# Attention times values in plain float32, two heads on the two column halves of TensorE

## The chip, the cores and the metric

The kernel runs on one core of a Trainium2 chip. A core has a matrix engine (TensorE, PE in the profile; its weight loads are PEld), three engines for elementwise work (VectorE or DVE, ScalarE or ACT, GpSimd or POOL), and SyncE (SP), which issues most of the DMA transfers. Each engine works through its own queue in order and waits on semaphores for the others. The metric is the device time of one execution in microseconds (us).

## The reference

One step of a streaming encoder layer. A prompt of 2048 frames and a sample of 8 x 16 frames, both 1024 wide, are normalised and projected by one input matrix; three groups of heads of width 64 read the result, and one output matrix merges them:

- A: 6 heads; a frame sees its own chunk of 64 frames and the 8 chunks before, with a learned bias by distance.
- B: 6 query heads on 2 key/value heads; own chunk and 2 chunks before, a linear distance bias, and a learned sink per head.
- M: 4 heads of cross-attention into 256 memory tokens.

```python
def _attn_core(q, k, v, bias, valid, sink):
    s = jnp.einsum('...qhgd,...khd->...hgqk', q, k).astype(jnp.float32) * SCALE
    ...
        p = jax.nn.softmax(s, axis=-1)
    ...
    return jnp.einsum('...hgqk,...khd->...qhgd', p.astype(v.dtype), v)


def _merge(x, oa, ga, ob, gb, om, gm, w_out, g_post):
    o = jnp.concatenate([oa * jax.nn.silu(ga), ob * jax.nn.silu(gb), om * jax.nn.silu(gm)], axis=-1) @ w_out
    return x + _rmsnorm(o, g_post)
```

All data are float32. The change is about the second einsum, p times v, for the prompt.

## The kernel before, in words

**Groups and steps.** The prompt is cut into 4 groups of 512 frames; group 0 also carries the 128 sample rows. In each group the kernel projects with the input matrix (`project_T`, line 191, gives 128 columns of q, k or a gate for all frames, transposed; `project_N`, line 202, gives rows of v, and the output projection), attends, and projects out. The order within a group is written out by hand in `ORDERS` (line 42): `V` projects values, `Pa`/`Pb` project q, k and gate of a pair of heads, `Aa`/`Ab`/`M` attend, `X` loads a pair's context, `L` loads and scales the next group's rows, `Q` projects the next group's M queries, `F` finishes the rows of the group before. A tile framework then schedules every engine's queue from this order with a simulated timeline, so later work can fill in where earlier work is not ready. The last part of a group is mostly attention, and the output projection follows it.

**Precision by splitting.** Most products run in the format that the code calls `F32R`. For them the code splits an operand into a high part (a copy to F32R) and a low part (the difference), and adds up products: three passes for a projection (high x high, high x low, low x high). Input weights are split by `load_w`: a DMA into `wraw`, a copy on ScalarE (line 139), a subtraction on VectorE or GpSimd (line 140), into one of three `whl` buffers.

**Attention of a pair of heads.** Two heads h = 0, 1 share a 128-partition tile, 64 rows each. For A the 512 queries are taken in two sub-steps of 2 x 128 (`for i0 in (0, 2)`); for B and M all 512 at once.
- Scores (line 241) go to PSUM, one tile `s` at a time. VectorE adds the bias and takes the minimum (lines 727, 798; 643 for M), ScalarE takes the exponential (729, 800, 648), VectorE scales by the reciprocal (732, 809, 653). The weights stand in `sb` tiles, of which there are five buffers.
- `transposed_p` turns up to four 128 x 128 blocks of one head on TensorE (line 247) into a PSUM tile `pt` (three buffers). Then `split`: ScalarE copies the high part (208), VectorE subtracts for the low part (209), both into one of three `pslot`s.
- Values are stored per head as 128 columns: high part and low part of 64 columns each, arranged so that head 0 has its high part in columns 0 to 63 and head 1 in columns 64 to 127. `attend` (line 260) multiplies the 128-column value block once with the high and once with the low weights, all into one PSUM tile `o`: two matmuls for each head and value block, of 256 columns (a block that two query tiles see) or 128 columns (one query tile).
- The two column halves of the result have to be added: `merge` copies one half to `sums` on ScalarE (267) and adds the other on VectorE (268), per head. `gate` multiplies `sums` with the SiLU gate on GpSimd (631) into `mo`.

**Output.** `split_mixed` (890 on VectorE, 891 on GpSimd) splits `mo` into `mixhl`, and `project_out` multiplies. The last group has its own code (lines 914 to 959) that begins the output projection before the last pair is done; it splits four output weight tiles ahead, two of them into spare room, two into `whl` buffers.

**One shared region.** `sh` (10496 columns) holds, at different times and overlapping, keys, four value slots, the three `pslot`s, the memory split `memhl` and `mixhl`. Context keys and values of A go to DRAM (`kctx_d`, `vctx_d`) and come back one group later by GpSimd's DMA queue (lines 840, 841).

**The sample rows** (`sample_attn`) already use plain float32: line 358 multiplies with 32-column stationary blocks, one for each of four sequences b, each into its own 32 partitions of the PSUM tile, and line 392 does the same for the values, for every block t of 128 cached frames. Line 385 transposes.

Of the kernel before, what the change touches and what calls it, by code (L numbers as in the profile page):

```python
# [9 lines left out]
F32 = mybir.dt.float32  # L10
# [39 lines left out]
def encoder_step(ctx, tc, x_p, x_s, xT0, xT, mem, memT, wt, wm, g_pre, g_mem, g_post, rel_rev, sink,  # L50
# [10 lines left out]
    sbp = ctx.enter_context(tc.tile_pool(name="sbp", bufs=5))  # L61
    cp_ = ctx.enter_context(tc.tile_pool(name="cp", bufs=1))
# [10 lines left out]
    sh = cst.tile([128, 10496], F32R, name="sh")  # L73
# [10 lines left out]
    def region(off, *dims):  # L84
        n = int(np.prod(dims))
        ap = sh[:, off:off + n]
        names = "abcde"[:len(dims)]
        if len(dims) > 1:
            pat = " ".join(names)
            ap = ap.rearrange(f"p ({pat}) -> p {pat}", **dict(zip(names[1:], dims[1:])))  # L90
        return ap


    keys = region(0, 2, 1664)
    kslot = [keys[:, :, 128 + 512 * i:640 + 512 * i] for i in range(3)]
    pslot = [region(7424 + 1024 * i, 2, 512) for i in range(3)]
    mixhl = region(0, 5, 2, KB, 128)
    memhl = region(0, 2, KB, 256)
    mixlast = xn[:, :8192].rearrange("p (i a k r) -> p i a k r", i=4, a=2, k=KB)
    turn = {"p": 0, "s": 0, "q": 0, "g": 0, "d": 0, "u": 0, "m": 0}  # L100

    def vregion(slot):
        return sh[:, 3328 + 1024 * slot:4352 + 1024 * slot].rearrange("p (a b) -> p a b", b=256)
# [17 lines left out]
    mV = cst.tile([128, 2, 2, 256], F32R, name="mV")  # L121
# [6 lines left out]
    vctx_d = [drp.tile([128, 4, 256], F32, name=f"vctx{i}") for i in range(6)]  # L128
# [55 lines left out]
    def project_T(w, src, c0, n, ps=None):  # L184

        if ps is None:
            ps = p_mm.tile([128, 512], F32, tag="mm", name="psT")
        i = 0
        for k in range(KB):
            for a, b in ((0, 0), (0, 1), (1, 0)):  # L190
                pe.matmul(ps[:, :n], w[:, a, k * 128:(k + 1) * 128], src[:, b, k, c0:c0 + n],  # L191
                          start=(i == 0), stop=(i == 23))
                i += 1
        return ps
# [48 lines left out]
    def transposed_p(blocks):  # L243
# [5 lines left out]
        dst = pslot[1 + turn["p"] % 2 if turn["m"] else turn["p"] % 3]  # L249
        turn["p"] += 1  # L250
        split(dst[:, 0, :n], dst[:, 1, :n], pt[:, :n])
        return dst

    def attend(o, items, first):

        n = 2 * len(items)
        i = 0
        for v, pt, c, w, oc in items:
            for part in range(2):
                pe.matmul(o[:, oc:oc + w], v, pt[:, part, c:c + w], start=(first and i == 0), stop=(i == n - 1),  # L260
                          skip_group_check=True)
                i += 1

    def merge(o, h, col, dst, n):

        m, x = slice(64 * h, 64 * h + 64), slice(64 - 64 * h, 128 - 64 * h)
        act.activation(dst[m, :n], o[x, col:col + n], AF.Copy)
        dve.tensor_tensor(dst[m, :n], o[m, col:col + n], dst[m, :n], ALU.add)  # L268
# [12 lines left out]
    def memory_rows(cols):  # L281

        for k in range(KB):
            act.activation(memhl[:, 0, k], cols[k], AF.Copy, scale=gmem[:, k:k + 1])
            dve.scalar_tensor_tensor(memhl[:, 1, k], cols[k], gmem[:, k:k + 1], memhl[:, 0, k].bitcast(F32),
                                     ALU.mult, ALU.subtract)
# [15 lines left out]
    def memory_keys(st):  # L302
# [11 lines left out]
        for i in range(2):  # L314
            ps = project_N(ws, lambda a, k: memhl[:, a, k, i * 128:(i + 1) * 128])
            split_v([mV[:, 0], mV[:, 1]], i, ps, st[:, i:i + 1])
# [175 lines left out]
    def project_out(ws, c, i, gpost, st):  # L492

        ps = project_N(ws, lambda a, k: mixhl[:, i, a, k])
# [22 lines left out]
    def xg(g):  # L517
        return xnT[min(g, 1)]
# [60 lines left out]
    mst = memory_rows(mT)  # L579
    qg.append((*block_q(0, 7, w7[0]), block_g(0, 7, w7[1])))  # L580
    memory_keys(mst)
# [5 lines left out]
    for g in range(NG):  # L587
# [14 lines left out]
        def block_v(slots, half):  # L602
            ws = [weights("v", half, r) for r in range(2)]
            for i in range(5 if g == 0 else 4):
                ps = project_N(ws, lambda a, k: xg(g)[:, a, k, i * 128:(i + 1) * 128])
# [9 lines left out]
                split_v(slots, i, ps, rs_rows[:, i:i + 1] if g == 0 else None)  # L615
# [12 lines left out]
        def gate(f, col, n, sums, G, g=g):  # L628

            dst = mom[:, f - 6, col // 128:(col + n) // 128] if f > 5 and g else mo[:, col // 128:(col + n) // 128, f]  # L630
            pool.tensor_tensor(dst, sums[:, :n].rearrange("p (a b) -> p a b", b=128),  # L631
                               G[:, col:col + n].rearrange("p (a b) -> p a b", b=128), ALU.mult)


        def attn_m(g, pr, q, Q, G):
            f = 6 + pr
            sums = cp_.tile([128, 512], F32, tag="sums", name="sums")
            for h in range(2):
# [5 lines left out]
                sbs = []  # L644
                for i2 in range(2):
# [8 lines left out]
                    sbs.append(sb)  # L654
                o = p_o.tile([128, 512], F32, tag="o", name="om")
                for i2 in range(2):
                    pt = transposed_p([sbs[i2][:, i * 256 + j * 128:i * 256 + (j + 1) * 128]
                                       for j in range(2) for i in range(2)])
# [428 lines left out]
```

## Time and profile before

| | |
|---|---|
| median of 3 runs | 1199.81 us (1195.86 to 1201.51) |
| the profiled execution, own time | 1199.29 us |
| its span | 1197.5 us |
| TensorE matmuls, busy | 1137.5 us, 95% |
| VectorE, busy | 840.0 us, 70% |
| ScalarE, busy | 689.5 us, 58% |
| GpSimd, busy | 362.2 us, 30% |

How to read it. A row of a group of instructions gives line, engine, operation, the tile written and the tiles read, the shapes, the count, then busy us and mean ns of one, then the idle time of the engine just before them and what ended it. Busy time by stage gives, for a stretch of the span, each engine's busy us and number of instructions, then TensorE's granted clock, the DMA share and GB/s. The chain of waits goes back from the last instruction to whatever released each step; its shares say which work set the end. In the timeline a row gives start, length, engine, line and count; matmuls overlap, so their pace is the distance of starts.

### The profile page before, as it was taken

How to read it: one execution, taken by the hardware profiler on the slowest of the kernel's cores; microseconds unless marked ns; L12 is line 12 of the kernel's file. 1: busy time of each engine (PE TensorE's matmuls, PEld its weight loads, DVE VectorE, ACT ScalarE, POOL GpSimd, SP SyncE). 2: the span in 40 equal slices, each digit the busy share in tenths (PEclk: the TensorE clock that was granted, in tenths of full speed). 3: DMA queues.
4: the chain of work that ended last, by engine and by line, in shares of the span. 5: the costliest groups of instructions: out<-in, count | busy, mean ns of one | idle time of the engine just before them, and what ended most of it. 6: DMA issues, size and time to landing. Idle time of an engine off the chain costs nothing.

```text
span 1197.5 us, 20992 instructions
## 1 busy us (share of the span) xinstructions
PE 1137.5 (95%) x7794; PEld 1024.5 (86%) x7794; DVE 840.0 (70%) x1911; ACT 689.5 (58%) x1609; POOL 362.2 (30%) x286
## 2 busy tenths in 40 slices
PE   7899999999989999999999999999988998999897
PEld 6789898897679988898888988898778987988797
DVE  7648666777784457779997336679997336679965
ACT  6546565655544565558664455557765444667652
POOL 5411210211261552122433552122333450221441
PEclk9899999999889999999999999999999998999999
DMA  7673552624621593333311493333321471432213
GB/s 264 211 226 130 172 181 57 232 83 151 240 71 53 176 341 119 110 111 112 126 58 36 133 360 115 111 114 123 115 63 36 129 285 54 126 97 89 90 54 106
DMA packets 62239, 163.43 MB, mean 136 GB/s; under 512 B 8109, under 2 KB 19379, under 8 KB 62137
## 3 DMA queue, kind: packets, MB, share of 16 engines
q1 hardware_dynamic: 58392, 152.66, 38.4%
q0 software_dynamic: 3744, 9.44, 2.7%
q8 instruction: 61, 1.00, 0.3%
q14 instruction: 42, 0.34, 0.1%
HBM read 140.95 MB, written 23.48 MB: 137 GB/s over the span
## 4 chain that ended last, share of the span: by engine, by line
PE 74%; DVE 16%; ACT 3%; issue 3%; DMA 2%; POOL 1%; SPq 0%; DVEq 0%; POOLq 0%; ACTq 0%
PE psT L191 33%; PE psN L202 23%; PE pt L247 5%; PE oa L260 4%; PE sa L241 3%; DVE sh L209 3%; DVE whl L140 1%; DVE sba L727 1%; PE om L260 1%; DVE sbb L798 1%; DVE sbb L809 1%; PE ss L358 1%; PE so L392 1%; PE ob L260 1%; PE sm L241 1%
## 5 line engine op out<-in xcount | busy, mean ns | idle before, releaser
L191 PE MATMUL psT<-xn,whl 128*128 128x512 f32 (+2 forms) x2400 | 531.8, 370 | 11.3 <-ACT whl L139 6.8
L191 PEld LDWEIGHTS psT<-xn,whl 128*128 128x128 f32 x2400 | 410.1, 192 | 73.9 <-ACT whl L139 7.1
L140 POOL TENSOR_TENSOR whl<-wraw,whl 128x1024 fp32r<-128x1024 f32 x64 | 155.7, 2433 | 357.5 <-ACT whl L139 303.7
L202 PE MATMUL psN<-whl,sh 128*128 128x256 f32 x1296 | 162.2, 283 | 1.5 <-POOL sh L891 1.3
L202 PEld LDWEIGHTS psN<-whl,sh 128*128 128x128 f32 x1296 | 156.4, 189 | 3.7 <-POOL sh L891 1.5
L139 ACT ACTIVATE whl<-wraw 128x1024 fp32r<-128x1024 f32 (+1 forms) x132 | 138.2, 1047 | 33.8 <-PE psN L202 13.7
L202 PE MATMUL psN<-whl,xn 128*128 128x256 f32 x1080 | 143.0, 283 | 3.1 <-ACT stgN L618 1.1
L202 PEld LDWEIGHTS psN<-whl,xn 128*128 128x128 f32 x1080 | 133.4, 189 | 7.2 <-issue 1.6
L209 DVE TENSOR_TENSOR sh<-pt,sh 128x512 fp32r<-128x512 f32 (+2 forms) x206 | 123.7, 625 | 21.5 <-ACT sh L208 20.5
L208 ACT ACTIVATE sh<-pt 128x512 fp32r<-128x512 f32 (+2 forms) x206 | 104.4, 547 | 41.0 <-PE pt L247 34.0
L729 ACT ACTIVATE sba<-sba,sta 128x640 f32<-128x640 f32 (+4 forms) x96 | 73.1, 761 | 65.8 <-DVE sta L727 64.0
L140 DVE TENSOR_TENSOR whl<-wraw,whl 128x1024 fp32r<-128x1024 f32 (+1 forms) x68 | 98.9, 1455 | 15.8 <-ACT whl L139 15.4
L631 POOL TENSOR_TENSOR mo<-sums,gr 128x256 f32<-128x256 f32 (+1 forms) x44 | 45.0, 1022 | 186.3 <-DVE sums L268 169.0
L727 DVE CUSTOM_DVE_ANT_0 sba<-sa,nbA 128x640 f32<-128x640 f32 (+4 forms) x96 | 70.6, 735 | 33.2 <-PE sa L241 32.4
L260 PE MATMUL oa<-sh 128*128 128x256 f32 (+1 forms) x504 | 82.0, 285 | 10.9 <-DVE sh L209 7.7
L260 PEld LDWEIGHTS oa<-sh 128*128 128x128 f32 x504 | 71.5, 192 | 17.0 <-DVE sh L209 9.6
L497 DVE TENSOR_TENSOR mo<-psN,gpost 128x256 f32<-128x256 f32 x52 | 22.1, 424 | 73.8 <-ACT junk L496 73.7
L247 PE MATMUL pt<-ident,sba 128*128 128x128 f32 x420 | 67.5, 281 | 3.4 <-DVE sba L732 3.2
L800 ACT ACTIVATE sbb<-sbb,stb 128x256 f32<-128x256 f32 (+1 forms) x96 | 47.3, 493 | 27.7 <-DVE stb L798 27.5
L732 DVE TENSOR_SCALAR sba<-sba,sta 128x640 f32<-128x640 f32 (+4 forms) x96 | 59.9, 624 | 2.6
L496 ACT ACTIVATE junk<-psN 128x256 bf16<-128x256 f32 x52 | 20.0, 384 | 62.3 <-PE psN L202 62.2
L247 PEld LDWEIGHTS pt<-ident,sba 128*128 128x128 f32 x420 | 49.6, 143 | 7.1 <-DVE sba L732 4.2
(282 smaller groups left out, 1643.9 us busy)
## 6 DMA issues: line engine op xcount, KB each, us to landing
wraw<-in_wt SPq DMA_DIRECT2D x128, 512.0 KB, 3.6
xr<-in_x_p SPq DMA_DIRECT2D x16, 512.0 KB, 5.8
nbA<-skew_d SPq DMA_DIRECT2D x24, 320.0 KB, 3.2
vta<-in_cva SPq DMA_DIRECT2D x12, 512.0 KB, 4.5
xt<-in_x_p SPq DMA_DIRECT2D x12, 512.0 KB, 5.0
out_y_p<-mo SPq DMA_DIRECT2D x12, 512.0 KB, 4.7
vctx<-sh SPq DMA_DIRECT2D x9, 512.0 KB, 5.4
kctx<-sh SPq DMA_DIRECT2D x9, 512.0 KB, 4.1
```

The source lines that it names most:

```text
L139: act.activation(hl[:, 0, m], raw[:, m], AF.Copy)
L140: eng.tensor_tensor(hl[:, 1, m], raw[:, m], hl[:, 0, m].bitcast(F32), ALU.subtract)
L191: pe.matmul(ps[:, :n], w[:, a, k * 128:(k + 1) * 128], src[:, b, k, c0:c0 + n], start=(i == 0), stop=(i == 23))
L202: pe.matmul(ps[:, :256], stat(a, k), w[:, b, (k % 4) * 256:(k % 4 + 1) * 256], start=(k == ks[0] and i == 0), stop=(k == ks[-1] and i == 2))
L208: act.activation(hi, src, AF.Copy)
L209: eng.tensor_tensor(lo, src, hi.bitcast(F32), ALU.subtract)
L241: pe.matmul(out[:, c:c + n], q[:, part, qc:qc + 128], kt[:, h, kc:kc + n], start=part == h, stop=part != h)
L247: pe.transpose(pt[:, i * 128:(i + 1) * 128], b, ident)
L260: pe.matmul(o[:, oc:oc + w], v, pt[:, part, c:c + w], start=(first and i == 0), stop=(i == n - 1), skip_group_check=True)
L727: dve.tensor_tensor_reduce(sb[:, :nk], s[:, c0:c0 + nk], nb[h][:, 640 - nk:], 1.0, 3.0e38, ALU.add, ALU.min, st[:, e:e + 1])
L729: act.activation(sb[:, :nk], sb[:, :nk], AF.Exp, bias=st[:, e:e + 1], scale=-1.0, accum_out=st[:, 2 + e:3 + e])
L732: dve.tensor_scalar(sb[:, :nk], sb[:, :nk], st[:, 4 + e:5 + e], 0.5, ALU.mult, ALU.mult)
```

## The change

The products of weights and values for the prompt take plain float32 operands. Nothing is split there: `transposed_p` only copies, `keep_v` stores the values once. The two heads' products go to the two column halves: head h uses the 64 value columns of its own as stationary block and writes partitions 64h to 64h + 63 of `o`. So the result needs no `merge`, and `gate` multiplies straight from PSUM, on VectorE. Blocks of both heads now share a transposed tile, all transposes of a step come first, and its matmuls follow in one run, the last tile's first.

Around it: the shared region `sh` is gone. Keys have a tile of their own; values of a group (`vall`), transposed weights (`pT`), `memhl` and the split mix share a pool `up` of five buffers; a fifth transposed tile of a step goes to `pTe`. V context is half as wide. The last group has one spare place for split weights instead of two. GpSimd's DMA scratch is halved. ORDERS, scores, softmax, projections and the sample path stay as they were.

```diff
+    up = ctx.enter_context(tc.tile_pool(name="up", bufs=5))
-    sh = cst.tile([128, 10496], F32R, name="sh")
+    keys = cst.tile([128, 2, 1664], F32R, name="keys")
...
-    def split_v(slots, i, ps, scale=None):
-        for s, v in enumerate(slots):
-            src = ps[:, 128 * s:128 * s + 128].rearrange("p (h d) -> p h d", h=2)
-            hi = v[:, i, :].rearrange("p (a d) -> p a d", d=64)[:, 0:4:3, :]
-            lo = v[:, i, :].rearrange("p (a d) -> p a d", d=64)[:, 1:3, :]
-            split(hi, lo, src, scale)
+    def keep_v(dst, i, ps, scale=None):
+        src = ps[:, :256].rearrange("p (s b) -> p s b", s=2)
+        if i % 2:
+            dve.tensor_copy(dst, src) if scale is None else dve.tensor_scalar(dst, src, scale, None, ALU.mult)
+        else:
+            act.activation(dst, src, AF.Copy, scale=1.0 if scale is None else scale)
...
-        split(dst[:, 0, :n], dst[:, 1, :n], pt[:, :n])
+        act.activation(dst[:, :n], pt[:, :n], AF.Copy)
...
-    def attend(o, items, first):
-        n = 2 * len(items)
-        i = 0
-        for v, pt, c, w, oc in items:
-            for part in range(2):
-                pe.matmul(o[:, oc:oc + w], v, pt[:, part, c:c + w], start=(first and i == 0), stop=(i == n - 1),
-                          skip_group_check=True)
-                i += 1
-
-    def merge(o, h, col, dst, n):
-        m, x = slice(64 * h, 64 * h + 64), slice(64 - 64 * h, 128 - 64 * h)
-        act.activation(dst[m, :n], o[x, col:col + n], AF.Copy)
-        dve.tensor_tensor(dst[m, :n], o[m, col:col + n], dst[m, :n], ALU.add)
+    def attend(o, entries, block, values):
+        pT = up.tile([128, 4, 512], F32, tag="u", name="pT")
+        items, part, width, n_parts = [], [], 0, 0
+        for j, qs, oc in entries:
+            dst = pT[:, n_parts] if n_parts < 4 else cp_.tile([128, 512], F32, tag="pTe", name="pTe", bufs=2) if width == 0 else dst
+            part += [block(h, j, i) for h in range(2) for i in qs]
+            items.append((values(j), dst, width, 128 * len(qs), oc))
+            width += 256 * len(qs)
+            if width == 512 or len(items) == len(entries):
+                transposed_p(part, dst)
+                part, width, n_parts = [], 0, n_parts + 1
+        for n, (v, pt, c, w, oc) in enumerate(reversed(items)):
+            for h in range(2):
+                pe.matmul(o[64 * h:64 * h + 64, oc:oc + w], v[:, 64 * h:64 * h + 64], pt[:, c + h * w:c + h * w + w],
+                          start=n == 0, stop=n == len(items) - 1, skip_group_check=True)
...
-            pool.tensor_tensor(dst, sums[:, :n].rearrange("p (a b) -> p a b", b=128),
-                               G[:, col:col + n].rearrange("p (a b) -> p a b", b=128), ALU.mult)
+            dve.tensor_tensor(dst, o[:, :n].rearrange("p (a b) -> p a b", b=128),
+                              G[:, col:col + n].rearrange("p (a b) -> p a b", b=128), ALU.mult)
...
+        vall = up.tile([128, 4, 4, 128], F32, tag="u", name="vall")
...
+            mix = [up.tile([128, 2, KB, 128], F32R, tag="u", name="mix") for _ in range(nrt)]
...
-        ws = [load_w(wt[W_AT["o", EARLY + j // 2, j % 2]], (room + [None] * 2)[j]) for j in range(4)]
+        ws = [load_w(wt[W_AT["o", EARLY + j // 2, j % 2]], None if j else room) for j in range(4)]
...
-    nc = bacc.Bacc("TRN2", target_bir_lowering=False, num_devices=1, dynamic_dma_scratch_size=4096)
+    nc = bacc.Bacc("TRN2", target_bir_lowering=False, num_devices=1, dynamic_dma_scratch_size=2048)
```

More of the change, by code (lines that the diff above doesn't have):

```diff
@@ L517, in xg @@
     def xg(g):
-        return xnT[min(g, 1)]
+        return [xnT[min(g, 1)][:, a] for a in range(2)]
     def columns(w, g, n0, n):
@@ L578, in encoder_step @@
     mT = memory_load()
-    mst = memory_rows(mT)
+    memhl = [up.tile([128, KB, 256], F32R, tag="u", name="memhl") for _ in range(2)]
+    mst = memory_rows(memhl, mT)
     qg.append((*block_q(0, 7, w7[0]), block_g(0, 7, w7[1])))
-    memory_keys(mst)
+    memory_keys(memhl, mst)
     for p in range(2):
@@ L781, in attn_b @@
                 sp.dma_start(out=nb[:, h], in_=nb_b[j0 + 3 * h])
[L782 removed]
+            sbs = {}
             for h in range(2):
```

172 lines of the change are left out of this document (60 added, 112 removed).

## The prediction

> **What bounds the kernel now.** I read the page first, then busy time by stage, then the chain of waits inside the stages that looked different, then the groups and the timeline of the TensorE instructions that change.
>
> ```profile
> span 1197.5 us, 20992 instructions
> PE 1137.5 (95%) x7794; PEld 1024.5 (86%) x7794; DVE 840.0 (70%) x1911; ACT 689.5 (58%) x1609; POOL 362.2 (30%) x286
> ...
> PE 74%; DVE 16%; ACT 3%; issue 3%; DMA 2%; POOL 1%; SPq 0%; DVEq 0%; POOLq 0%; ACTq 0%
> ...
> L140 POOL TENSOR_TENSOR whl<-wraw,whl 128x1024 fp32r<-128x1024 f32 x64 | 155.7, 2433 | 357.5 <-ACT whl L139 303.7
> ...
> L139 ACT ACTIVATE whl<-wraw 128x1024 fp32r<-128x1024 f32 (+1 forms) x132 | 138.2, 1047 | 33.8 <-PE psN L202 13.7
> L209 DVE TENSOR_TENSOR sh<-pt,sh 128x512 fp32r<-128x512 f32 (+2 forms) x206 | 123.7, 625 | 21.5 <-ACT sh L208 20.5
> ...
> wraw<-in_wt SPq DMA_DIRECT2D x128, 512.0 KB, 3.6
> ```
>
> TensorE is busy 95% and carries 74% of the chain that ended last; VectorE carries 16%, which is 192 us of 1197.5. An average of 70% busy for VectorE does not fit that share, so the question is where the 16% lies. Busy time by stage answers it:
>
> ```profile
> core 0: us, PE busy (x) PEld busy (x) DVE busy (x) ACT busy (x) POOL busy (x), PEclk, DMA share, GB/s
> ...
> 360.00:550.00 190.00, 190.00 (x1284) 174.44 (x1283) 116.47 (x247) 104.30 (x228) 58.50 (x39) 1.00 0.44 148
> 550.00:630.00 80.00, 76.25 (x474) 67.36 (x473) 76.16 (x177) 58.85 (x141) 27.16 (x26) 0.98 0.32 100
> ...
> 800.00:910.00 110.00, 101.48 (x614) 87.94 (x613) 104.48 (x240) 73.22 (x183) 33.09 (x31) 0.98 0.27 87
> ...
> 1070.00:1165.00 95.00, 90.12 (x604) 81.27 (x603) 82.05 (x207) 62.03 (x154) 33.31 (x32) 0.98 0.27 85
> ```
>
> For 190 us from 360 on TensorE never rests and VectorE is at 61%. In the last part of each of the groups 1, 2 and 3 the picture turns: the projections have been used up as cover, attention is left, and VectorE is busy 95%, 95% and 86% while TensorE shows 3.75, 8.52 and 4.88 us of idle time, 17.2 in all. Two different limits, then. The chain of waits in these three stretches (550 to 630, 800 to 910, 1070 to 1165) names the work:
>
> ```profile
> by line: PE psT L191 18.5%; DVE sh L209 9.6%; DVE sbb L798 6.3%; PE pt L247 6.1%; DVE sbb L809 5.7%; DVE sba L727 4.9%; issue 4.0%; PE oa L260 3.9%; DVE sums L268 3.3%; DVE qr L219 3.3%; PE sm L241 3.1%; PE psN L202 2.9%; DVE whl L140 2.8%;
> ```
> ```profile
> by line: PE psT L191 16.3%; DVE sh L209 10.7%; issue 6.2%; DVE sbm L653 5.3%; DVE sbb L798 5.2%; DVE sbb L809 4.6%; DVE xk L176 4.2%; DVE sba L727 3.6%; ACT sbb L800 3.5%; DVE stm L643 3.2%; DVE whl L140 3.0%; ACT sbm L648 2.8%; DVE qr L220
> ```
> ```profile
> by line: PE psN L202 17.7%; PE psT L191 14.5%; DVE sh L209 7.5%; PE oa L260 7.2%; PE pt L247 5.4%; DVE xn L890 4.9%; issue 4.4%; DVE sba L727 3.9%; DVE sbb L809 3.5%; PE ob L260 3.0%; DVE whl L140 2.8%; ACT sbb L800 2.6%; PE sa L241 2.5%; D
> ```
>
> L209 is the subtraction that makes the low part of the transposed weights, and it is VectorE's largest entry in all three.
>
> **VectorE: what goes and what comes.** The change drops every L209 that reads `pt`: 206 instructions, 123.7 us. It drops the addition of the two halves, L268:
>
> ```profile
> L268 DVE TENSOR_TENSOR sums<-oa,sums 64x256 f32<-64x256 f32 x48 | 20.2, 420 | 11.6 <-ACT sums L267 10.8
> ...
> L268 DVE TENSOR_TENSOR sums<-ob,sums 64x512 f32<-64x512 f32 x24 | 16.4, 684 | 0.4
> ...
> L268 DVE TENSOR_TENSOR sums<-om,sums 64x512 f32<-64x512 f32 x16 | 11.0, 685 | 5.8 <-ACT sums L267 5.5
> ```
>
> That is 47.6 us more. It adds the gate product, which moves from GpSimd to VectorE: 24 of 256 columns and 20 of 512. Priced by the L268 rows of the same width, which also read PSUM, this is 24 x 0.42 + 20 x 0.685 = 23.8 us. Net, VectorE loses about 147 of its 840 us. In the three stretches L209 takes
>
> ```profile
> 550.00:630.00 80.00, 18.39 (x29) 6.85 (x4) 0.98 0.32 100
> ...
> 800.00:910.00 110.00, 21.27 (x34) 5.20 (x4) 0.98 0.27 87
> ...
> 1070.00:1165.00 95.00, 18.22 (x30) 0.00 (x0) 0.98 0.27 85
> ```
>
> (VectorE first, GpSimd second; a few of these belong to other tiles). VectorE's 262.7 us of 285 fall to about 205, or 72%, so it stops being the limit there.
>
> What is that worth? On the chain, L209 has 9.6% of 80 + 10.7% of 110 + 7.5% of 95 = 7.7 + 11.8 + 7.1 = 26.6 us, and L268 another 2.6 us in the first stretch: 29.2 us at most by these rows. At least, TensorE's visible idle time, 17.2 us, stands against it; a matmul record outlasts the start of its successor, so short stalls do not show as idle and the true slack is larger. Nothing at all comes back if a new wait takes its place: now the blocks of both heads go into one transposed tile, so all four `sb` tiles of a step are held until its last transposes, out of five buffers, and the gate sits in VectorE's queue behind the last matmul of the step, with the next step's L727 or L798 behind it. VectorE waited at that place before (11.6 + 0.4 + 5.8 = 17.8 us in the L268 rows). Between 0 and 29 I take 20, near the visible idle time, because the four-tile hold costs some but VectorE is no longer full.
>
> Edits priced at nothing. ScalarE keeps one copy for each transposed tile (206 become 188) and loses L267; at 58% overall and at most 74% in the three stretches it was not the limit. Splitting the values, two copies and two subtractions for each row tile, becomes one copy, hidden under projections as before; uncovered, a copy is about 0.42 us (L268's width). GpSimd loses 44 gates, so the weight splits queued behind them (L140) come earlier; they are not on TensorE's path while the projections run without a pause. The V context transfers halve, at a DMA share below a half. GpSimd's descriptor space is halved too, which no row prices; its context loads are
>
> ```profile
> sh<-kctx POOLq DMA_DIRECT2D x9, 512.0 KB, 4.9
> ```
>
> and stand at least a projection ahead of their attention, so a second load that waited for the first would be 4.9 us later and still under cover. The separate homes for keys, values and the split mix remove write-after-read waits only; what they might give is in the last rival.
>
> **TensorE: the products.** The instructions replaced are
>
> ```profile
> L260 PE MATMUL oa<-sh 128*128 128x256 f32 x336 | 63.7, 296 | 10.9 <-DVE sh L209 7.7 <-DVE sums L268 3.0 <-ACT sh L208 0.2
> ...
> L260 PE MATMUL oa<-sh 128*128 128x128 f32 x168 | 26.2, 261 | 0.0
> L260 PE MATMUL ob<-sh 128*128 128x256 f32 x144 | 23.7, 293 | 0.2 <-DVE sums L268 0.2
> ...
> L260 PE MATMUL om<-sh,mV 128*128 128x256 f32 x128 | 18.8, 284 | 0.3 <-DVE sums L268 0.3
> ...
> L260 PE MATMUL ob<-sh 128*128 128x128 f32 x48 | 8.2, 253 | 0.0
> ...
> L260 PE MATMUL ob<-sh,bv 128*128 128x128 f32 x36 | 6.9, 275 | 0.0
> ```
>
> 608 of 256 columns and 252 of 128. Their pace is read from starts, not durations, in the timeline of TensorE, together with plain-float32 products that the sample path already runs on parts of the columns:
>
> ```profile
> 440.16 1.10 PE L260 MATMUL om<-sh,mV 128*128 128x256 f32 x8
> 441.09 5.75 PE L191 MATMUL psT<-xn,whl 128*128 128x512 f32 x24
> ```
> ```profile
> 1116.37 0.39 PE L260 MATMUL ob<-sh,bv 128*128 128x128 f32 x2
> 1116.59 0.41 PE L247 MATMUL pt<-ident,sbb 128*128 128x128 f32 x2
> ```
> ```profile
> 59.40 0.64 PE L358 MATMUL ss<-mo,qd 128*32 128x256 f32 x8
> 59.97 0.51 PE L202 MATMUL psN<-whl,sh 128*128 128x256 f32 x2
> ```
> ```profile
> 131.59 0.60 PE L385 MATMUL spt<-ident,ssb 128*128 128x128 f32 x4
> 132.12 1.05 PE L358 MATMUL ss<-mo,qd 128*32 128x512 f32 x4
> 133.10 0.79 PE L191 MATMUL psT<-xn,whl 128*128 128x384 f32 x3
> ```
> ```profile
> 147.74 1.08 PE L392 MATMUL so<-vta,spT 128*32 128x128 f32 x32
> 148.75 0.51 PE L241 MATMUL sa<-sh,qr 128*128 128x256 f32 x2
> ```
>
> Before: 0.93 / 8 = 0.116 us each at 256 columns, 0.22 / 2 = 0.11 at 128; 608 x 0.116 + 252 x 0.11 = 98 us.
>
> After: L392 loops over 16 products and the row has 32 records, so a float32 product is two records. At 132.12, two products of 512 columns on two column groups (four records) are over 0.98 us later; at 59.40, four of 256 columns on four groups in 0.57. The difference, 0.41, is two passes of 256 more columns: 0.205 a pass for 256, 0.1025 for 128, and products on different column groups share a pass. What is left is 0.57 - 0.41 = 0.16 for a run of two passes and 1.01 - 0.82 = 0.19 for one of eight: a cost of the run, not of the pass. Entering costs about 0.09 (0.53 for the four records at 131.59, against 0.11 each). So 0.27 a run. The change makes of four old matmuls one pair of two passes: 152 pairs of 256 and 63 of 128, in 24 + 12 + 8 = 44 runs (sub-steps of A, B and M). 304 x 0.205 + 126 x 0.1025 + 44 x 0.27 = 62.3 + 12.9 + 11.9 = 87 us, 11 less than before. If other matmuls cut into a run, each cut costs 0.27 again; with some 18 cuts I take -6. The count of transposes does not change.
>
> The upper bound: if the 0.16 were weight loading, paid in each pass (0.08), 430 passes cost 34.4 in place of 7.5, 114 us in all, 15 more than before. The nearest row, the run of eight passes, speaks for the lower end. The Trainium skill's "TensorE: Matmul & The Clock Gate", Part 3 (What overlaps and what doesn't) says that a weight load overlaps a running matmul only if their row groups differ; both halves here use all rows, so by it every pass would pay. By that rule the sum would be the 15 us more; the 0.19 of the eight-pass run does not bear it out.
>
> **The tail.** The last group loses one spare place for split weights, so four splits share three buffers: the fourth waits for the `last` weights' readers. It costs at most a load, a copy and a subtraction: 3.6 + 1.05 + 2.43, near 7 us by the rows above; the matmuls of other row tiles can run meanwhile. I take +1.
>
> **Sum.** -20 - 6 + 1 = -25 on the profiled execution's 1199.29 us (0.5 below the median 1199.81): **1174**.
>
> **Rivals.**
> *The wait comes back.* With both heads needed before the first transpose, the next step's reductions wait for `sb` tiles and VectorE's gate waits for TensorE. For: 4 of 5 buffers held. Against: it was 4 of 5 in A before too, released a half earlier. Of the 20 some 4 stay and the runs are cut more often (PE 0): about 1196.
> *Weight loads exposed*, above: -20 + 15 + 1, about 1195.
> *The halves run in turn* (slower). If two products of 64 columns do not share a pass, the passes double: 62.3 + 12.9 = 75 us more on TensorE, 1249. Against it: the overlapping pair at 132.12. For: no row has 64-column halves. It decides against the change once a third of the pairs (25 / 75) fail to overlap; the change would then not do what it says.
> *More than forecast*: the whole 29 and the whole 11, with waits on the shared region gone: about 1157.
>
> **Numbers.** Forecast 0.62, wait comes back 0.16, loads exposed 0.08, halves in turn 0.07, more 0.07. A measurement of this kernel can tell about 0.5%, that is 6 us. Faster: 0.60 of the forecast, 0.07, and 0.08 from the two rivals that lie near 1195, 0.75; within: 0.15; slower: the halves in turn and a little of the others, 0.10. The range goes from 1150 (the large case, with its unknowns) to 1205 (both near rivals, with 10 us on top); it leaves out the halves in turn and the edges.
>
> **What would show it.** Right: no `pt` subtraction; VectorE near 690 us; in the ends of groups VectorE below 80% and TensorE's idle time mostly gone; records of 64 columns in pairs that start together, near 0.21 us a pass at 256. Wrong: pair starts 0.2 us apart, VectorE idle before L727 and L798 on the gate, or TensorE still idle in the same three stretches.

## The result and the profile after

The changed kernel takes **1249.0 us** in the median (1243.7 to 1251.0), beside 1199.5 for the kernel before: a ratio of 1.041, 95% interval 1.0369 to 1.045. The forecast was 1174 and its range ended at 1205; the sign is wrong.

In the page of the changed kernel three engines stand as forecast: VectorE fell by 138.5 us (147 forecast), and ScalarE and GpSimd lost work too. TensorE's busy time, which was to fall a little, rose by 12.2 us:

```profile
span 1247.5 us, 20345 instructions
PE 1149.7 (92%) x7794; PEld 988.0 (79%) x7794; DVE 701.5 (56%) x1610; ACT 634.5 (51%) x1452; POOL 312.4 (25%) x242
```

The pairs also run as priced. In the timeline of TensorE (start, length, engine, line, count) a sub-step of A reads:

```profile
639.54 0.66 PE L254 MATMUL oa<-pTe,vall 128*64 128x128 f32 x8
640.03 1.90 PE L254 MATMUL oa<-pT,vall 128*64 128x256 f32 x16
641.86 0.33 PE L232 MATMUL pt<-ident,sba 128*128 128x128 f32 x1
```

From the first product to the next other matmul are 641.86 - 639.54 = 2.32 us for 4 passes of 128 columns and 8 of 256. The prediction's prices give 4 x 0.1025 + 8 x 0.205 + 0.27 = 2.32. Had each of the 12 passes paid a weight load of 0.08 us, it would be near 3.1. The Trainium skill's "TensorE: Matmul & The Clock Gate", Part 3 (What overlaps and what doesn't) says that a weight load overlaps a running matmul only if the row groups differ, by which every pass here would pay; the 2.32 us do not bear it out.

The span is 50 us longer, and TensorE's two parts of it account for that: its idle time (span less busy) went from 60.0 to 97.8 us, its busy time up by 12.2. The busy part may be the clock. The mean granted clock is 0.979 before and 0.971 after; the share not granted is then 0.021 x 1197.5 = 25.1 and 0.029 x 1247.5 = 36.2 us, 11 us more. That is an estimate, and no run tests it by itself. The rest is about the idle time. Busy time by stage, for the same four stretches as in the prediction, each moved by as much as the stage it precedes has moved (columns as there):

```profile
core 0: us, PE busy (x) PEld busy (x) DVE busy (x) ACT busy (x) POOL busy (x), PEclk, DMA share, GB/s
380.00:570.00 190.00, 188.45 (x1253) 166.78 (x1252) 91.68 (x173) 92.79 (x186) 52.28 (x32) 1.00 0.42 138
574.00:654.00 80.00, 68.51 (x403) 52.83 (x400) 62.21 (x153) 50.38 (x123) 21.92 (x23) 0.99 0.33 102
828.00:938.00 110.00, 98.09 (x603) 78.57 (x602) 79.75 (x196) 65.66 (x160) 28.72 (x27) 0.98 0.31 93
1120.00:1215.00 95.00, 83.68 (x586) 69.93 (x585) 58.08 (x167) 52.59 (x137) 24.71 (x26) 0.93 0.21 66
```

In the three ends of groups VectorE is down to 78%, 73% and 61%, under the 80% that the prediction named. But TensorE is idle 11.5, 11.9 and 11.3 us there, 34.7 in place of 17.2. Both engines rest at once: neither is the limit, each waits for the other. The waits name the places (engine, line, waited for: us in total, times, longest):

```profile
DVE sba L711 <- PE pt L232: 21.2, 8, 6.3
DVE sbb L761 <- PE pt L232: 21.2, 7, 5.3
DVE mo L619 <- PE oa L254: 17.1, 10, 4.1
DVE mo L619 <- PE om L254: 10.2, 5, 3.3
DVE mo L619 <- PE ob L254: 10.2, 6, 3.9
```

L711 and L761 are the reductions that open a softmax (L727 and L798 before). They write a fresh `sb` tile, so a wait for the transposes L232 is a wait for such a tile to come free. Of these 42.4 us, 2.1, 7.3 and 15.4 lie in the three stretches and 17.6 outside them, so in the first stretch other waits hold TensorE as well (4.1 us of its transposes for the softmax of M, L640). The kernel before hardly knew it, as its group for the same reduction shows, ahead of that of the changed kernel:

```profile
L727 DVE CUSTOM_DVE_ANT_0 sba<-sa,nbA 128x640 f32<-128x640 f32 x72 | 58.9, 818 | 29.3 <-PE sa L241 28.8 <-PE pt L247 0.2
```
```profile
L711 DVE CUSTOM_DVE_ANT_0 sba<-sa,nbA 128x640 f32<-128x640 f32 x72 | 59.2, 822 | 55.9 <-PE sa L226 31.0 <-PE pt L232 21.2 <-DMA out_akT<-stgT 1.6
```

There is a second place, early in group 0. TensorE projects the first two row tiles of the values until 74 us and goes on with the third only at 102.84; ScalarE copies the first one out at 102.49, without a wait, because the copy stands in its queue behind the softmaxes of M:

```profile
70.24 2.51 PE L187 MATMUL psN<-whl,xn 128*128 128x256 f32 x19
...
102.84 1.39 PE L187 MATMUL psN<-whl,xn 128*128 128x256 f32 x10
```
```profile
102.49 0.47 ACT L220 ACTIVATE vall<-psN,nst 128x256 f32<-128x256 f32 x1
```

Until then both PSUM banks for projections are taken and M runs without cover.

### The profile page after: what moved, and what is told of

Same layout as the page of the kernel before. It is cut to its first block, busy times and chain, and to the rows that moved or that the text cites. A ratio compares the mean times of both kernels' runs of the same rounds, so it can differ in the third digit from the quotient of the medians.

```text
span 1247.5 us, 20345 instructions
## 1 busy us (share of the span) xinstructions
PE 1149.7 (92%) x7794; PEld 988.0 (79%) x7794; DVE 701.5 (56%) x1610; ACT 634.5 (51%) x1452; POOL 312.4 (25%) x242
## 5 line engine op out<-in xcount | busy, mean ns | idle before, releaser
L176 PE MATMUL psT<-xn,whl 128*128 128x512 f32 (+2 forms) x2400 | 525.6, 370 | 21.6 <-ACT whl L124 7.0
L187 PE MATMUL psN<-whl,mix 128*128 128x256 f32 x1248 | 160.8, 289 | 1.9 <-DVE mo L484 1.6
L187 PEld LDWEIGHTS psN<-whl,mix 128*128 128x128 f32 x1248 | 155.7, 196 | 4.3 <-DVE mo L484 2.1
L187 PE MATMUL psN<-whl,xn 128*128 128x256 f32 x1128 | 149.9, 288 | 3.3 <-ACT whl L124 1.2
L187 PEld LDWEIGHTS psN<-whl,xn 128*128 128x128 f32 x1128 | 141.1, 193 | 8.2 <-issue 2.2
L234 ACT ACTIVATE pT<-pt 128x512 f32<-128x512 f32 (+1 forms) x170 | 90.7, 585 | 70.1 <-PE pt L232 69.5
L711 DVE CUSTOM_DVE_ANT_0 sba<-sa,nbA 128x640 f32<-128x640 f32 (+4 forms) x96 | 70.9, 739 | 61.1 <-PE sa L226 35.9
L232 PE MATMUL pt<-ident,sba 128*128 128x128 f32 x420 | 67.2, 280 | 7.6 <-DVE sba L716 5.0
L232 PEld LDWEIGHTS pt<-ident,sba 128*128 128x128 f32 x420 | 50.2, 142 | 18.9 <-DVE sba L716 6.5
L226 PE MATMUL sa<-keys,qr 128*128 128x320 f32 (+4 forms) x240 | 52.0, 327 | 10.4 <-DVE sta L711 6.8
L226 PEld LDWEIGHTS sa<-keys,qr 128*128 128x128 f32 x240 | 38.3, 191 | 20.4 <-DVE sta L711 10.1
L635 ACT ACTIVATE sbm<-sm,stm 128x256 f32<-128x256 f32 x64 | 29.6, 477 | 37.3 <-DVE stm L631 37.0
L254 PE MATMUL oa<-pT,vall 128*64 128x256 f32 (+1 forms) x360 | 42.0, 374 | 1.2 <-ACT pT L234 1.2
```

The lines of the kernel that those rows point to most:

```text
L176: pe.matmul(ps[:, :n], w[:, a, k * 128:(k + 1) * 128], src[b][:, k, c0:c0 + n], start=(i == 0), stop=(i == 23))
L187: pe.matmul(ps[:, :256], stat(a, k), w[:, b, (k % 4) * 256:(k % 4 + 1) * 256], start=(k == ks[0] and i == 0), stop=(k == ks[-1] and i == 2))
L226: pe.matmul(out[:, c:c + n], q[:, part, qc:qc + 128], kt[:, h, kc:kc + n], start=part == h, stop=part != h)
L232: pe.transpose(pt[:, i * 128:(i + 1) * 128], b, ident)
L234: act.activation(dst[:, :n], pt[:, :n], AF.Copy)
L254: pe.matmul(o[64 * h:64 * h + 64, oc:oc + w], v[:, 64 * h:64 * h + 64], pt[:, c + h * w:c + h * w + w], start=n == 0, stop=n == len(items) ...
```

## The experiments

My theory was **the hold**: both heads' `sb` tiles stay taken until the last transposes. The rivals: **the order and the queues** (copies of values, gate, projections standing behind them) and, for group 0, **the shared ring** (values, transposed weights and split mix in one pool of five). Every edit also makes the framework lay out all queues anew. All kernels compute the whole reference. Ratios are to the kernel before, run beside each (1197.1 to 1200.7 us). Differences in us are between medians; taken from the ratios they move by up to 4 us.

**e1, six `sb` tiles.**

```diff
-    sbp = ctx.enter_context(tc.tile_pool(name="sbp", bufs=5))
+    sbp = ctx.enter_context(tc.tile_pool(name="sbp", bufs=6))
...
-... name="pTe", bufs=2) ...
+... name="pTe", bufs=1) ...
```

> The changed kernel (1249.0) with a sixth `sb` tile in the pool of weight tiles; the room comes from the second buffer of the fifth part `pTe`. Theory 'the hold': the tiles of both heads, four of five, stay taken until the last transposes of a sub-step, so the next softmax finds no tile. Then the waits of VectorE's L711 and L761 on the transposes (21.2 + 21.2 us) shrink to a few us and the time falls to 1205 to 1230. Theory 'the order and the queues': the loss lies in keep_v, the gate and the projections that stand behind them in the queues; then one tile more changes less than 6 us, 1244 to 1254.

Measured 1210.1 us, 1.0087 (1.0069 to 1.0106): 39 us back, inside what the hold expected. Of VectorE's waits for transposes one is left:

```profile
DVE sba L711 <- PE pt L232: 7.9, 3, 5.2
```

In the three ends of groups, moved along as before, TensorE's idle time is 17.4 us (75.05, 104.24 and 88.35 us busy of 80, 110 and 95), where the changed kernel has 34.7 and the kernel before 17.2.

**e10, four `sb` tiles** (`bufs=4`, nothing else).

> The changed kernel with four `sb` tiles in place of five: now the two heads of a sub-step take all of them. 'The hold': a step as large as that from five to six (39) or larger, 1280 to 1310. Without the hold: within 6 us of 1249.

Measured 1261.7, 1.053 (1.0499 to 1.0561): 13 us more, the right direction but under the expected 31 to 61.

```profile
DVE sba L711 <- PE pt L232: 28.2, 10, 7.4
DVE sbb L761 <- PE pt L232: 22.4, 6, 7.9
```

The waits are 50.6, 42.4 and 7.9 us with four, five and six tiles; the large step is the sixth. That five leave one tile for the next step, and six a pair, fits this, but was only argued.

**e6, the kernel before with six tiles** (the same edit of `sbp` there).

> The kernel before with a sixth `sb` tile and nothing else. 'The hold is the change's': the kernel before frees two tiles of four a head earlier and does not need the sixth, within 4 us of 1199.5. If tiles were short before as well: 1170 to 1190, and the gain of the sixth tile says nothing of the change.

Measured 1207.5, 1.0087 (1.0065 to 1.0109). The old kernel gains nothing, so the sixth tile repairs something that the change broke. It even loses 10 us, which neither theory expected; nothing but the layout of the queues differs. I take 10 us as what a new layout can do by itself, and put no cause on smaller differences.

**e2, head order**: all blocks of head 0 transposed and copied, then those of head 1, so head 0's tiles come free early; the products in pairs, in forward order.

```diff
-            part += [block(h, j, i) for h in range(2) for i in qs]
...
+        for h in range(2):
...
+                    part += [block(h, entries[k][0], i) for i in entries[k][1]]
...
+                transposed_p(part, dst)
```

> The changed kernel with the transposes ordered by head: all blocks of head 0, their copies, then those of head 1; the products still run in pairs at the end. Head 0's `sb` tiles come free as soon as its own transposes are done. In A six copies of a bank instead of five. 'The hold': 1185 to 1220, since no tile of head 0 waits for head 1 any more. 'The order and the queues': 1243 to 1254, or a little slower for the 32 added copies.

Measured 1221.7, 1.0183 (1.0157 to 1.0209): 27 us back, between the two expectations. TensorE's idle time falls from 97.8 to 56.9 us (e1: 70.7), but its busy time rises from 1149.7 to 1164.2: the products are now cut into 98 runs. What that costs is the matter of e13 and e17.

**e3, values in a buffer of their own.**

```diff
-    up = ctx.enter_context(tc.tile_pool(name="up", bufs=5))
+    up = ctx.enter_context(tc.tile_pool(name="up", bufs=4))
+    vp = ctx.enter_context(tc.tile_pool(name="vp", bufs=1))
...
-        vall = up.tile([128, 4, 4, 128], F32, tag="u", name="vall")
+        vall = vp.tile([128, 4, 4, 128], F32, tag="v", name="vall")
```

(The fifth `mix` of group 0 takes this buffer when the values are done.)

> The changed kernel with the values `vall` in a buffer of their own and four buffers (not five) for pT, mix and the memory rows. In the trace of the changed kernel the first two row tiles of V0 are projected by 73 us and copied out only at 102, after M0's products have released their pT, and TensorE stands idle meanwhile. 'The shared ring': the copies move up to about 75 us, V0 runs among the softmaxes of M0 and M1, and the first group ends 8 to 15 us earlier: 1234 to 1241. 'The hold' alone: 1244 to 1254.

Measured 1226.6, 1.022 (1.0195 to 1.0245): 22 us back, more than expected. Busy time in the stretch in question, the changed kernel first, then e3:

```profile
60.00:80.00 20.00, 17.57 (x182) 14.77 (x179) 9.48 (x23) 7.91 (x19) 2.40 (x1) 0.97 0.81 256
80.00:100.00 20.00, 14.37 (x82) 11.59 (x82) 10.64 (x27) 8.42 (x30) 0.00 (x0) 0.60 0.23 81
100.00:120.00 20.00, 19.36 (x153) 17.35 (x150) 6.58 (x14) 8.07 (x19) 2.40 (x1) 1.00 0.23 76
```
```profile
60.00:80.00 20.00, 20.00 (x199) 18.16 (x202) 8.81 (x18) 8.35 (x18) 2.77 (x2) 1.00 0.71 231
80.00:100.00 20.00, 20.00 (x183) 18.66 (x171) 13.59 (x25) 8.22 (x21) 4.80 (x2) 1.00 0.59 195
100.00:120.00 20.00, 20.00 (x150) 19.01 (x148) 14.63 (x37) 13.43 (x40) 1.30 (x1) 1.00 0.24 78
```

The hole is gone: the first copy now stands at 72.19, and V0 runs among the softmaxes:

```profile
72.19 0.48 ACT L221 ACTIVATE vall<-psN,nst 128x256 f32<-128x256 f32 x1 [0.28 <-PE psN L188]
```

That the shared pool put the copy so late is shown by this exchange; by which rule of the framework is not.

**e5, both remedies** (e1 and e3 together).

> The changed kernel with both remedies: a sixth `sb` tile and the values in a buffer of their own. If the hold (-39 in the run with six tiles) and the shared ring (-22 in the run with values of their own) are two separate causes, they add: 1249 - 39 - 22 = 1188, range 1180 to 1196, below the kernel before. If they are one cause seen twice: 1205 to 1212.

Measured 1183.9, **0.9886** (0.9864 to 0.9907): the two add up, and the kernel is faster than the one before. In the whole span TensorE is busy 1127.5 us and idle 54.6. In the stretches ahead of the ends of groups TensorE's idle time is 5.0 + 5.7 + 6.5 = 17.3 us, that of the kernel before:

```profile
535.00:615.00 80.00, 75.00 (x458) 60.10 (x457) 63.21 (x155) 52.39 (x128) 24.04 (x24) 0.97 0.35 109
780.00:890.00 110.00, 104.26 (x659) 84.67 (x659) 86.00 (x203) 67.45 (x164) 33.94 (x31) 0.98 0.35 110
1056.00:1151.00 95.00, 88.46 (x609) 74.66 (x608) 61.33 (x169) 55.46 (x142) 23.61 (x26) 0.96 0.25 79
```

**e8, the gate off VectorE** in the changed kernel, as it was before. The room for `sums` comes from the second buffer of `pTe`.

```diff
-            dve.tensor_tensor(dst, o[:, :n].rearrange("p (a b) -> p a b", b=128),
+            sums = cp_.tile([128, 512], F32, tag="sums", name="sums")
+            act.activation(sums[:, :n], o[:, :n], AF.Copy)
+            pool.tensor_tensor(dst, sums[:, :n].rearrange("p (a b) -> p a b", b=128),
```

> The changed kernel with the gate as before the change: ScalarE copies the products to an SBUF tile and GpSimd multiplies, so that VectorE's queue no longer waits for the products (37.5 us of idle time ahead of L619 in the changed kernel). 'The gate in VectorE's queue': 1215 to 1238. 'The hold' and 'the shared ring' without it: 1244 to 1254, since VectorE is then idle for want of work anyway.

Measured 1229.7, 1.0268 (1.0244 to 1.0293): 19 us back, as "the gate in VectorE's queue" expected.

**e9, the gate off VectorE on top of e5** (ScalarE copies into `mo`, GpSimd multiplies there).

> The kernel with six `sb` tiles and values of their own (1183.9), and the gate taken off VectorE: ScalarE copies the products straight into `mo`, GpSimd multiplies there. If the gate in VectorE's queue is a third cause, as the -19 of the gate alone says, it adds: 1160 to 1172. If the gate alone gained only because VectorE was held by the missing tiles, nothing is left of it: 1180 to 1192.

Measured 1184.2, 0.9874 (0.9845 to 0.9903): nothing is left of the 19. So the gate is no third cause beside the two remedies. That it costs only while VectorE is held at the same place by the missing tiles is my reading; the two edits also differ in where ScalarE copies to.

**e4, products of head 0 all ahead of head 1's.**

```diff
-        for n, (v, pt, c, w, oc) in enumerate(reversed(items)):
-            for h in range(2):
+        for h in range(2):
+            for n, (v, pt, c, w, oc) in enumerate(reversed(items)):
```

> The changed kernel with the products of head 0 all ahead of those of head 1, so that neighbours are on the same column half. If the pairs do run side by side in the changed kernel, TensorE gets up to 75 us more (62.3 + 12.9): 1290 to 1325 where nothing hides it. If the halves already ran in turn there, the rival that I gave 1249: within 6 us of 1249.

**e11, the same with values of their own.** It was meant to stand on e5, and its expectation is for that; but the kernel that ran has five `sb` tiles and two `pTe` buffers, so it is e3 with this edit.

> The kernel with six `sb` tiles and values of their own, with the products of head 0 all ahead of those of head 1. In the changed kernel the same edit cost 29 us, where TensorE had idle time to hide it in. If the remedies gave TensorE back to the work, the edit costs more of its 75 here: 1220 to 1245. If as much is hidden as before: 1210 to 1216.

Measured 1278.2, 1.0652 (1.0629 to 1.0675), 29 more than the changed kernel, under the 41 to 76 expected; and 1261.6, 1.0528 (1.0499 to 1.0557), 35 more than e3. The ranges of e11, for six tiles, cannot be held against it. So the halves did not run in turn in the changed kernel. TensorE's busy time grew by 39 us in e4 (1149.7 to 1188.5) and 45 in e11 (1143.1 in e3 to 1188.6), not by 75. The same run of 16 records in the changed kernel and in e4 shows why:

```profile
98.77 2.18 PE L254 MATMUL om<-pT,mV 128*64 128x256 f32 x16
100.87 0.33 PE L232 MATMUL pt<-ident,sbm 128*128 128x128 f32 x1
```
```profile
99.45 3.37 PE L254 MATMUL om<-pT,mV 128*64 128x256 f32 x16
102.75 0.88 PE L232 MATMUL pt<-ident,sbm 128*128 128x128 f32 x6
```

2.10 us become 3.30, not twice as much: head 1's first products start on their half while head 0's last still run. (Both runs fall partly into a stretch at half clock; the other runs of M with 16 records take 1.88 us in pairs and 2.79 in turn. In one of the latter the records start one by one, 0.215 us apart, except from 0.92 to 1.62 us into the run, where they start two by two.) The side-by-side order is worth 29 to 35 us in kernels with five tiles; with six it was not run.

**e12, VectorE's removed work put back into e5.**

```diff
         act.activation(dst[:, :n], pt[:, :n], AF.Copy)
+        dve.tensor_tensor(dst[:, :n], pt[:, :n], dst[:, :n], ALU.max)
```

> The kernel with six `sb` tiles and values of their own, and VectorE's removed work put back: after ScalarE's copy of each transposed bank VectorE takes the larger of the bank and the copy, which are equal, into the copy, 188 instructions of the shapes of the removed subtractions (some 126 us), and the products wait for it. The prediction's term (VectorE's relief is worth 20, between 0 and 29): 1198 to 1213. Relief worth nothing by itself: 1178 to 1190. Relief worth more than its bound: above 1213.

Measured 1227.6, 1.0233 (1.0204 to 1.0263): 44 us more than e5, beyond the prediction's bound of 29. The instructions took

```profile
L236 DVE TENSOR_TENSOR pT<-pt,pT 128x512 f32<-128x512 f32 x161 | 105.1, 682 | 27.5 <-ACT pT L235 27.1
```

and 16.0 us in two smaller groups (12.3 for `pTe`), with a wait of 27 us ahead of them. So putting the work back costs 44 us here, the load and the step on the way to the products together, which this run does not separate. It is not what taking the work out gave: the kernel before had the same copy and subtraction on the way and was idle on TensorE for 60.0 us, this one for 81.7.

**e13 and e14, products in forward order**, on e5 and on the changed kernel. In reverse, the first product needs the last copied bank, so all follow in one run; forward, each may start with its own bank.

```diff
-        for n, (v, pt, c, w, oc) in enumerate(reversed(items)):
+        for n, (v, pt, c, w, oc) in enumerate(items):
```

> The kernel with six `sb` tiles and values of their own, with the products in the order of the parts and no longer in reverse. In reverse the first product needs the last transposed bank, so none starts before all banks are copied; in order, each starts with its own bank. 'The products stand at the end': the latency of the last copy and the wait of the gate shrink, 1160 to 1176. If the run in one piece was no cost (or the cuts cost 0.27 us each, some 100 more of them): 1180 to 1212.

> The changed kernel with nothing but the products in the order of the parts. 'The products stand at the end' as a cause by itself: 1225 to 1240. If the hold and the shared ring are what matters: 1243 to 1255, since products that start earlier free no `sb` tile and no values.

Measured 1213.1, 1.0132 (1.0096 to 1.0168), 29 more than e5, above its second range too; and 1237.8, 1.0341 (1.0307 to 1.0374), 11 less than the changed kernel and inside the range of its first theory, that the products at the end cost by themselves. The timeline of e13 shows the runs cut to pieces:

```profile
627.56 0.66 PE L233 MATMUL pt<-ident,sba 128*128 128x128 f32 x4 [0.47 <-ACT pT L235]
628.15 0.65 PE L255 MATMUL oa<-pT,vall 128*64 128x256 f32 x4
628.73 0.66 PE L233 MATMUL pt<-ident,sba 128*128 128x128 f32 x4
629.32 0.65 PE L255 MATMUL oa<-pT,vall 128*64 128x256 f32 x4
629.90 0.39 PE L188 MATMUL psN<-whl,mix 128*128 128x256 f32 x1
```

One pair takes 0.58 us (628.15 to 628.73) in place of 2 x 0.205. Counted over all 860 records of the products in the two timelines, e5 has 46 runs and e13 119; the times from the first product of a run to the next other matmul add up to 87.4 and 104.9 us. That is 17.5 of the 29 us. The one run is a gain of the change's design once TensorE is busy. In e14 VectorE's waits for the transposes at L711 and L761 are 15.0 and 5.3 us in place of 21.2 and 21.2, TensorE is idle 77.5 us in place of 97.8 and busy 1157.3 in place of 1149.7: cuts cost there too, but about half of the hold's waits went. Why they went I did not settle, and 11 us is about the size that a new layout makes, so this rival is neither shown nor excluded.

**e7, e15: head order in forward order with values of their own**, with five and with six tiles (e2 + e3, and e1 besides).

> The changed kernel with transposes ordered by head and the values in a buffer of their own, still five `sb` tiles. If the two causes add: 1249 - 27 - 22 = 1200, range 1192 to 1208; if they are one: 1218 to 1227.

> Head by head (transposes and copies of head 0 first, products in order at the end), six `sb` tiles, values of their own. If six tiles and head order cure the same hold: 1180 to 1190, no better than six tiles alone. If head order had cured something else (the products' start): 1165 to 1178. If its six copies for five in A cost something: 1190 to 1215.

Measured 1214.1, 1.0143 (1.0114 to 1.0171), between its two ranges; and 1220.8, 1.019 (1.0146 to 1.0234), above all three, nearest to that of a cost. Both had 100 runs of products in place of 46. So the two were made again in one run:

**e16, e17: head order in one run**, with six and with five tiles.

```diff
-        for n, (j, qs, oc) in enumerate(entries):
+        for n in reversed(range(len(entries))):
+            j, qs, oc = entries[n]
...
-            for h in range(2):
+            for h in (1, 0):
```

> As the run with head order, six `sb` tiles and values of their own (1220.8), with the products in reverse and head 1's first, so that they stand in one run again: that kernel had 100 runs of products in place of 46, 118 us from the first product to the next other matmul in place of 87. If the cuts were what it lost: 1180 to 1195, and below 1180 if head order frees tiles that six alone do not. If its sixth copy and the later products were what it lost: 1210 to 1225.

> The same with five `sb` tiles. If head order cures the hold as six tiles do, once the cuts are gone: 1180 to 1195. If it does not: 1210 to 1226, the level of values of their own alone.

Measured 1197.0, 0.9966 (0.9941 to 0.9991), just above the range that the cuts alone allowed, and 1190.4, **0.9917** (0.9885 to 0.9949). With five tiles, head order takes 36 us off e3 (1226.6), nearly what the sixth tile takes off it (43, e5); VectorE no longer waits for the transposes at either reduction. Two cures that share only the freeing of tiles do the same thing, and both together do no more. The hold is shown.

**e18, two product banks** (`p_o` 2, `p_t` 2 in place of 1 and 3) on e16.

> The first of these two with two PSUM banks for the products and two (not three) for the transposes. If the single product bank, which must wait for the gate of the step before, holds the products: 8 to 15 us below that run. If the third transposed bank is worth more: above it.

Measured 1182.0, 0.9844 (0.9811 to 0.9876): 15 us below e16, at the upper edge of its range, and level with e5. Its ratio is the lowest of all, but it is not below e5's by more than runs of the two can tell.

## Why the prediction was wrong, point by point

**The step that failed** is "Between 0 and 29 I take 20, near the visible idle time, because the four-tile hold costs some but VectorE is no longer full." It set the price of the new waits inside the gain: the worst case was that "nothing at all comes back". A hold doesn't ask how full VectorE is. It stops the next softmax, TensorE then runs out of work, and both rest at once. It cost 36 (e17) to 43 us (e5), more than the 20 it was set against and more than the 29 that was the most the term could give. No bound below zero was set for it.

The 20 itself is not shown either. In e5, with the hold and the ring cured, VectorE stands at 79, 78 and 65% in the three stretches, and TensorE is idle there for 17.3 us as before. So a VectorE that is no longer full did not by itself give the visible idle time back; e12 prices that work at 44 us within e5, which is another question.

**The rival "the wait comes back"** had the mechanism right and the size wrong, for the same reason: 1196 assumed that 16 of the 20 are lost and nothing beyond. Its argument against itself, "it was 4 of 5 in A before too, released a half earlier", was true for A and left out B and M, where the old kernel held two tiles; and the half earlier is, as I read it, what the 21.2 us at L711 wait for: e17, which gives it back, has no such wait.

**"What they might give is in the last rival"**, of the separate homes, missed that the change also puts values, transposed weights and mix into one pool. That cost 22 us alone (e3) and 26 beside six tiles (1210.1 to 1183.9). **"Hidden under projections as before"**, of the value copies, failed at that place: the copy at 102.49 stopped the very projections that were to hide it.

Taken together: 1249.0 - 39 - 26 = 1184, e5 (the second step is measured on the first, so the sum holds by itself; that the two add rests on 26 beside 22). The two causes are the whole loss against the kernel before, and 14 us more (1197.7 beside e5).

**TensorE's products** were priced right, in size (2.32 us for 2.32; 87.4 over all runs in e5, 87 forecast) and as a run that should not be cut (e13). The products of the kernel before were priced too low: counted in the same way over its trace they stand in 187 runs and take 111.5 us, where the prediction has 98 without cuts, so they shrank by 24 and not by 11. The rival **"weight loads exposed"** falls with this. **"The halves run in turn"** named 1249, which is the measured time, but by a mechanism that isn't there: in pairs the passes are shared, and put in turn they cost 29 and 35 us more (e4, e11). A number that fits shows nothing by itself.

**VectorE's busy time** was right, and its wrong sign too: "VectorE idle before L727 and L798 on the gate" happened (37.5 us at L619 in all), but as a companion of the hold (e8, e9). Its last sign, "TensorE still idle in the same three stretches", came true as well (34.7 us). **The tail** (+1) and the halved DMA scratch were not tried by themselves.

**Open:** what the change is worth with the hold and the ring cured. By its span e5 is 15.4 us shorter than the kernel before: TensorE is busy 10.0 us less and idle 5.4 us less. The products alone shrank by 24 us and VectorE's work by over 130, so most of both does not arrive. TensorE is idle at the ends of groups as long as before, 17.3 us. The longer way to the first product (two heads' softmax, transposes and copies) is my guess; e18 speaks for a part at the product bank, and no run isolates the rest.

## What to carry to other kernels

When a change makes several tiles be needed at once, count for every step that does so how many of the pool's buffers are left for the next step, and price the missing one by the whole stall behind it, not by the gain it stands against. Where tiles that live for a whole group share a pool with tiles that live for one step, try pools of their own (22 to 26 us here). If two engines go idle in the same stretch, look for a buffer that both wait for: here values in a buffer of their own, with one more tile or with tiles freed a head earlier, turned 4.1% slower into 1% faster.

## What the hardware showed that I had not expected

The granted clock fell in a stretch in which TensorE was never idle for long. In the changed kernel, between 84 and 96 us:

```profile
84.00:88.00 4.00, 2.98 (x15) 2.50 (x14) 2.56 (x9) 0.79 (x4) 0.00 (x0) 0.70 0.40 131
88.00:92.00 4.00, 1.90 (x10) 1.79 (x10) 2.05 (x7) 1.93 (x8) 0.00 (x0) 0.50 0.00 0
92.00:96.00 4.00, 2.55 (x11) 1.75 (x10) 1.85 (x4) 3.17 (x11) 0.00 (x0) 0.50 0.00 0
```
```profile
85.20 0.41 PE L232 MATMUL pt<-ident,sbm 128*128 128x128 f32 x2 [1.02 <-DVE sbm L640]
...
90.18 0.69 PE L232 MATMUL pt<-ident,sbm 128*128 128x128 f32 x2 [2.10 <-DVE sbm L640]
```

The clock was 0.90 from 84 to 86 and 0.50 from 86 to 88, so it fell near 86, and no pause of TensorE between 72 and that point was longer than the 1.02 us ahead of 85.20. From 88 to 96 it stayed at half clock (0.50), with TensorE busy 48% and 64% of the time and no pause longer than 2.10 us; in e3 the clock was 1.00 from 60 to 120. The matmuls between the pauses were slow as well (two transposes in 0.69 us, where e13 shows four in 0.66), so a hole in the cover was paid twice. The Trainium skill's "TensorE: Matmul & The Clock Gate", Part 1 (What's actually happening), lets an idle window of about 3.4 us halve the clock; these rows show it without a pause of that length.

And plain-float32 products on the two column halves overlap even when issued one head after the other: 16 records took 2.79 us in turn and 1.88 in pairs at full clock, where 16 passes of 0.205 one after the other would take 3.28.
